# A hybrid RG-LRU, convolution, Fourier and SSD block: SSD by channels before the output projection, projections as slots between the stages

## The chip, the cores and the metric

The kernel runs on one core of a Trainium2 chip. The metric is the device time of one launch in microseconds (us). The engines are TensorE (PE in the profile, its weight loads PEld), VectorE (DVE), ScalarE (ACT), GpSimd (POOL) and SyncE (SP), on whose queue every DMA of both kernels is issued. SBUF holds 128 partitions; PSUM is used as eight banks of 128x512 float32, two to each of four names (`mm`, `tr`, `ba`, `bb`).

## The reference

2048 tokens of 1024 channels (x) and 256 context tokens (ctx), one layer. Both are normed and modulated, projected, handled by four branches of 512 channels, gated, concatenated and projected back:

```
h = rmsnorm(x) * (1 + scale) + shift          # scale, shift, gate = adaln(c)
rg_x, ssd_xbc, ssd_dt, rg_g, ssd_z, sc_b, sc_c, sc_x, sc_g, fn_x, fn_g = split(h @ w_in)
y_rg  = rglru(conv4(rg_x))                    # two directions, from the context's states
y_sc  = sc_b * conv3(sc_c * sc_x)             # in rows of 64 tokens
y_fn  = real(fft2(fn_x))                      # over tokens and 128 channels of 4 groups
# SSD: xs, B, C = silu(conv4(ssd_xbc)); dt = softplus(ssd_dt + bias); cs = cumsum(dt * a)
# in chunks of 128 tokens, 8 heads of 64 channels, 2 groups of B and C of 64 states, two directions:
y     = ((C B^T) * exp(cs_i - cs_j) masked) @ (xs * dt) + exp(cs) * (C @ entering state)
y_ssd = rmsnorm((y_fwd + y_bwd + D * xs) * silu(z)) * ssd_norm_w
out   = rmsnorm(x + gate * (concat(y_rg * silu(rg_g), y_sc * silu(sc_g),
                                   y_fn * silu(fn_g), y_ssd) @ w_out))
```

The context is projected for the RG-LRU, xbc and dt only, and gives the states from which the scans of the tokens start. Everything is float32.

## The kernel before, in words

Large products are made of three of reduced operands: `split` rounds a tile on ScalarE to a high part (`copy_hi`, the profile's L139) and subtracts it on VectorE or GpSimd for the low part (L214); `mm3` (L142 to L144) then issues high by high, high by low and low by high. `proj` makes a tile of 128 channels by 512 tokens in 24 such products from a weight block (`wload`) and the normed, transposed tokens `h_hi`, `h_lo`, which stay in SBUF.

The program text goes through the stages one after another: adaLN, the tokens `h`, and beside them the RG-LRU's input columns and the context's columns (`rgx_out`, raw columns to memory); the RG-LRU in units of 512 tokens, whose convolution stands in `rg_front` (L521 to L523) ahead of its gates' products; z and dt in token order, 128 tokens by 264 columns (`wz`); the xbc columns with convolution and silu (`conv_silu`, `xbc_emit`); the SSD's step sizes, decays and chunk states, of which the states from the right are passed on at this point (`states`, L678); Fourier mixing; the first SSD chunk; the short convolution; the gates; the output weights (`wo_raw`, `wo_hi`, `wo_lo`); and the output projection (`oproj`, L1153 to L1155), one block of 128 tokens after another.

The SSD's chunks are in token order. `ssd_head` computes the scores (L982), the decays from `ci`, a row of the cumulative sums broadcast to all partitions (L1022 to L1033), and the part of the entering state (L1004 and L1005, from `hs`); `ssd_tail` multiplies the masked scores `ma` with `xs` (L1044), adds, gates, norms the rows and transposes the result by TensorE (L1060) for the output projection. In the loop over the output's 16 token blocks `ssd_chunk` is called one block ahead (`NEARLY = 1`), so a chunk's head and tail lie between the products of blocks.

The kernel is built with `schedule_with_timeline_sim=True`: the program text gives the dependences and a preference, and a scheduler that simulates the engines sets the order of each engine's instructions. Buffers come from pools: a tile with `bufs=2` has two places, and a third use waits for the first one's readers. Each engine runs its instructions in the order so set.

## Time and profile before

| | |
|---|---|
| three runs | 1654.54, 1656.22, 1657.36 us (median 1656.22) |
| profiled execution, span | 1656.3 us |
| TensorE busy | 1569.4 us, 95% |
| VectorE busy | 1053.3 us, 64% |
| ScalarE busy | 714.9 us, 43% |
| GpSimd busy | 564.3 us, 34% |
| moved by DMA | 220.93 MB, mean 133 GB/s |

A row of the stage table gives the length of a stretch and then, engine by engine, how long it was busy in it; the clock behind it is the share of TensorE's full speed that was granted (1.0 is 2.4 GHz, 0.5 is 1.2 GHz). The timeline gives start and duration of instructions; since products overlap in TensorE's pipeline, the distance between two starts is the price of one, not its duration. A row of waits names the waiting instruction and the one it waited for.

### The profile page before, as it was taken

The numbers are of one execution on the slowest core, as the hardware profiler recorded it, in microseconds if no ns is written. First come the engines' busy times: TensorE is split into PE (matmuls) and PEld (weight loads), VectorE is DVE, ScalarE is ACT, GpSimd is POOL, SyncE is SP. The second block draws the span as 40 slices with busy tenths as digits, with TensorE's granted clock in tenths as the row PEclk, the third lists the DMA queues.
The fourth block names the chain that finished last, engine by engine and source line by source line (L and its number), as shares of the span: only waits on it lengthen the run. The fifth ranks groups of instructions, "written<-read, shape, count | busy, mean of one in ns | idle before, by whom it ended". The sixth has DMA issues, their size and how long they took to land. (4 is left out here: it accounts for less than half of the span.)

```text
span 1656.3 us, 22749 instructions
## 1 busy us (share of the span) xinstructions
PE 1569.4 (95%) x7906; PEld 1271.5 (77%) x7906; DVE 1053.3 (64%) x1837; ACT 714.9 (43%) x1383; POOL 564.3 (34%) x536
## 2 busy tenths in 40 slices
PE   6899999899899999899999999898988999999998
PEld 3687899777788778666788888785766777777787
DVE  7765354698986657644168653437468777878653
ACT  5654046557465536211222324424345544545432
POOL 5533123312211422343315345334423424243310
PEclk9999999999999999999999999999999999999999
DMA  8424232323332231454222236657575655555532
GB/s 328 153 87 135 87 99 92 106 90 104 124 116 71 83 121 58 148 156 128 77 79 61 87 109 179 174 161 233 165 254 171 183 146 171 146 170 148 162 105 70
DMA packets 182257, 220.93 MB, mean 133 GB/s; under 512 B 20183, under 2 KB 118905, under 8 KB 182142
## 3 DMA queue, kind: packets, MB, share of 16 engines
q1 hardware_dynamic: 182142, 219.48, 42.8%
q8 instruction: 62, 1.02, 0.3%
q14 instruction: 53, 0.43, 0.1%
HBM read 155.40 MB, written 64.03 MB: 132 GB/s over the span
## 5 line engine op out<-in xcount | busy, mean ns | idle before, releaser
L142 PE MATMUL ps_mm<-h_hi,whi 128*128 128x512 f32 x696 | 276.9, 401 | 5.6 <-ACT craw L347 4.5
L143 PE MATMUL ps_mm<-h_lo,whi 128*128 128x512 f32 x696 | 278.7, 400 | 1.8 <-DVE h_lo L309 1.0
L144 PE MATMUL ps_mm<-h_hi,wlo 128*128 128x512 f32 x696 | 278.3, 400 | 0.0
L142 PEld LDWEIGHTS ps_mm<-h_hi,whi 128*128 128x128 f32 x696 | 133.1, 192 | 36.2 <-ACT craw L347 5.4
L143 PEld LDWEIGHTS ps_mm<-h_lo,whi 128*128 128x128 f32 x696 | 133.3, 192 | 31.6 <-DVE h_lo L309 2.2
L144 PEld LDWEIGHTS ps_mm<-h_hi,wlo 128*128 128x128 f32 x696 | 133.6, 192 | 28.9 <-issue 1.4
L142 PE MATMUL ps_tr<-h_hi,whi 128*128 128x512 f32 x384 | 151.6, 395 | 0.0
L143 PE MATMUL ps_tr<-h_lo,whi 128*128 128x512 f32 x384 | 151.5, 395 | 0.0
L144 PE MATMUL ps_tr<-h_hi,wlo 128*128 128x512 f32 x384 | 151.1, 394 | 0.0
L1153 PE MATMUL ps_mm<-wo_hi,oyhl 128*128 128x512 f32 (+1 forms) x272 | 106.9, 393 | 7.5 <-ACT oyhl L139 7.5
L139 ACT ACTIVATE whi<-wraw 128x512 fp32r<-128x512 f32 (+1 forms) x77 | 49.6, 645 | 143.4 <-DMA wraw<-wblk 98.4
L1155 PE MATMUL ps_mm<-wo_hi,oyhl 128*128 128x512 f32 (+1 forms) x272 | 106.2, 391 | 2.8 <-DVE oyhl L214 2.7
L1154 PE MATMUL ps_mm<-wo_lo,oyhl 128*128 128x512 f32 (+1 forms) x272 | 106.9, 393 | 0.0
L1009 POOL TENSOR_TENSOR y<-y,e 128x256 f32<-128x256 f32 x32 | 35.6, 1114 | 195.3 <-DVE e L1008 195.3
L1154 PE MATMUL ps_tr<-wo_lo,oyhl 128*128 128x512 f32 (+1 forms) x256 | 100.4, 392 | 0.0
L1155 PE MATMUL ps_tr<-wo_hi,oyhl 128*128 128x512 f32 (+1 forms) x256 | 100.0, 390 | 0.0
L1153 PE MATMUL ps_tr<-wo_hi,oyhl 128*128 128x512 f32 (+1 forms) x256 | 99.1, 387 | 0.0
L214 POOL TENSOR_TENSOR wlo<-wraw,whi 128x512 fp32r<-128x512 f32 (+1 forms) x40 | 61.7, 1543 | 97.3 <-ACT whi L139 81.8
L142 PEld LDWEIGHTS ps_tr<-h_hi,whi 128*128 128x128 f32 x384 | 72.8, 190 | 16.8 <-issue 2.1
L143 PEld LDWEIGHTS ps_tr<-h_lo,whi 128*128 128x128 f32 x384 | 72.6, 189 | 16.4 <-issue 1.7
L144 PEld LDWEIGHTS ps_tr<-h_hi,wlo 128*128 128x128 f32 x384 | 72.6, 189 | 15.6 <-issue 1.1
L139 ACT ACTIVATE oyhl<-oyr 128x512 fp32r<-128x512 f32 x68 | 42.6, 627 | 96.2 <-PE ps_tr L1155 72.6
(365 smaller groups left out, 3847.9 us busy)
## 6 DMA issues: line engine op xcount, KB each, us to landing
wraw<-wblk SPq DMA_DIRECT2D x74, 256.0 KB, 3.0
oyr<-ycat SPq DMA_DIRECT2D x68, 256.0 KB, 3.4
ci<-cst_d SPq DMA_DIRECT2D x64, 256.0 KB, 3.5
xs<-xsb_d SPq DMA_DIRECT2D x31, 320.0 KB, 3.0
adar<-ada SPq DMA_DIRECT2D x16, 512.0 KB, 10.2
hf_d<-r_v SPq DMA_DIRECT2D x32, 256.0 KB, 2.2
ycat<-gy SPq DMA_DIRECT2D x32, 256.0 KB, 2.4
wo_raw<-wout SPq DMA_DIRECT2D x16, 512.0 KB
```

The source lines that it names most:

```text
L139: act.activation(dst, src, AF.Copy)
L142: pe.matmul(ps, wh, xh, start=start, stop=False)
L143: pe.matmul(ps, wh, xl, start=False, stop=False)
L144: pe.matmul(ps, wl, xh, start=False, stop=stop)
L214: eng.tensor_tensor(lo, raw, f32(hi), SUB)
L1009: pool.tensor_tensor(y[:, s], y[:, s], e[:, 0:256], ADD)
L1153: pe.matmul(p, yhl[:, 0, j], wo_hi[q][:, j, c0:c1], start=first and j == 0, stop=False)
L1154: pe.matmul(p, yhl[:, 0, j], wo_lo[q][:, j, c0:c1], start=False, stop=False)
L1155: pe.matmul(p, yhl[:, 1, j], wo_hi[q][:, j, c0:c1], start=False, stop=last and j == 3)
```

## The change

Seven things change.

- The RG-LRU's convolution moves from `rg_front` to `rgx_out`, so the start phase stores convolved columns `u_d`; `rg_front` only loads them.
- dt is made by channels from a small weight `wdt` (`dt_of`, both parts of the weight side by side in 32 columns). z is four more weight blocks whose tiles get the gate at once and go to `dz_d` by channels; `xbc_emit` stores `D * xs` beside them.
- The weight blocks behind the RG-LRU's and the context's, with their gates, become a list of `jobs` (the last two stand behind the chunks, as `lastgate` jobs of their own), and the generator `slots` gives one tile of 512 tokens after another. `along` takes the steps of a stage (RG-LRU, states, Fourier, chunks) and issues as many slots between them as the step's number says.
- `keep_in_program_order` exists for TensorE's instructions, but `inorder` is False throughout, so the scheduler sets TensorE's order as before.
- The states of both directions are passed on in one pass (`step`), and each chunk's entering states are stored (`hin_d`).
- The chunk is by channels (`Chunk`): the outputs are 64 channels by 128 tokens, two heads to a bank's upper and lower partitions; entering states come in as `er` by `hin`, where `er` is a broadcast row of `exp(cs)` times C; the norm's sum over channels is a product with ones, and its power goes back by a transpose. No transposes of the output are left.
- All chunks stand before the output projection; the pool of the output weights' raw tiles (`qy`) is opened after the chunks' pool is closed, and the first four token blocks go by weight quarters.

```diff
+        inorder = False
+        def matmul(self, *a, **k):
+            i = nc.tensor.matmul(*a, **k)
...
+    def rgx_out(p, n, blk, dst, at, end):
+        raw = qe.tile([128, 516], F32, name="ev", tag="ev", bufs=2)
+        act.activation(raw[:, 3:3 + n], p[:, :n], AF.Copy)
+        if at == 0:
+            pool.memset(raw[:, 0:3], 0.0)
+        else:
+            dve.tensor_copy(raw[:, 0:3], rgc[blk])
+        m = n
+        if at + n == end:
+            pool.memset(raw[:, n + 3:n + 4], 0.0)
+            m = n + 1
+        else:
+            dve.tensor_copy(rgc[blk], raw[:, n:n + 3])
+        wc = [cols[:, C_RGW + 4 * k + blk:C_RGW + 4 * k + blk + 1] for k in range(4)]
+        u = qe.tile([128, 516], F32, name="ru", tag="ru", bufs=1)
+        act.activation(u[:, 0:m], raw[:, 2:2 + m], AF.Identity, scale=wc[2], bias=cols[:, C_RGB + blk:C_RGB + blk + 1])
+        for k in (0, 1, 3):
+            dve.scalar_tensor_tensor(u[:, 0:m], raw[:, k:k + m], wc[k], u[:, 0:m], MUL, ADD)
+        o = int(at == 0)
+        st(dst[:, at - 1 + o:at - 1 + m], u[:, o:m])
+    def rgx(w, blk, hh, hl, n, dst, at, end):
+        rgx_out(proj(w, hh, hl, n, False), n, blk, dst, at, end)
...
+    def dt_of(hh, hl, n, c0):
+        m = n // 128
+        p = bank("ba")
+        for k in range(8):
+            pe.matmul(p[0:32, :n], dtw[:, k], hh[:, k], start=k == 0, stop=False)
+            pe.matmul(p[0:32, :n], dtw[:, k], hl[:, k], start=False, stop=k == 7)
...
+    def zgate(j):
+        def at(tt, w):
+            p = proj(w, h_hi[tt], h_lo[tt])
+            st(dz_d[tt][1, j], gate(p, q3))
+        return [(B_Z + j, at)]
...
+    jobs = [j for i in range(4) for j in zgate(i)]
+    jobs += [j for i in range(2) for j in shortconv(i)]
+    at_xbc = 4 * len(jobs)
+    jobs += [j for i in range(6) for j in xbc(i)]
+    jobs += [j for i in range(2, 4) for j in shortconv(i)]
+    jobs += [j for i in range(4) for j in lastgate(B_RGG + i, hf_d[i], i)]
+    jobs += [j for i in range(2) for j in lastgate(B_FNG + i, (yp_d, yq_d)[i // 2][i % 2], 8 + i)]
+    ready = [wload(jobs[0][0])]
+    def slots():
+        for i, (b, at) in enumerate(jobs):
+            w = ready.pop()
+            for tt in range(4):
+                at(tt, w)
+                if tt == 0:
+                    ready.append(wload(jobs[i + 1][0] if i + 1 < len(jobs) else B_FNG + 2))
+                done[0] += 1
+                yield
+    bulk = slots()
+    owed, done = [0.0], [0]
+    def upto(n):
...
+    def along(steps):
+        for n in steps:
+            owed[0] += n
+            while owed[0] >= 1:
+                owed[0] -= 1
+                next(bulk, None)
...
-        for blk, d, g, src, conv, keep, init in us:
-            if conv:
-                # two columns before and one after, zero beyond the ends
...
-                wc = [cols[:, C_RGW + 4 * k + blk:C_RGW + 4 * k + blk + 1] for k in range(4)]
-                dve.tensor_scalar(u[:, d, :n], e2[:, d, 2:2 + n], wc[2], cols[:, C_RGB + blk:C_RGB + blk + 1], MUL, ADD)
-                for k in (0, 1, 3):
-                    dve.scalar_tensor_tensor(u[:, d, :n], e2[:, d, k:k + n], wc[k], u[:, d, :n], MUL, ADD)
-                if keep is not None:
-                    st(keep, u[:, d, :n])
...
-            for b in range(16):
-                hh, hl = h_hi[b // 4], h_lo[b // 4]
-                s = slice(128 * (b % 4), 128 * (b % 4) + 128)
-                zp = mbank(True)
-                for k in range(8):
-                    mm3(zp[:, :264], hh[:, k, s], hl[:, k, s], *wzs[k], k == 0, k == 7)
-                zt = qz.tile([128, 264], F32, name="zt", tag="zt", bufs=2)
-                o = 8 * half
-                act.activation(zt, zp[:, 0:264], AF.Copy)
-                pool.tensor_copy(dtr[:, 2 + b, o:o + 8], zt[:, 256 * (1 - half):256 * (1 - half) + 8])
-                st(z_d[b][:, 256 * half:256 * half + 256], zt[:, o:o + 256])
...
-        mas = []
-        for g in range(2):
-            cs2 = []
-            for d in range(2):
-                ci = sd.tile([128, 4, 128], F32, name="ci", tag="ci", bufs=3)
...
+            ci = d2("ci", (4, 2, 128), bufs=3)
+            ld(ci, cst_d[rows].rearrange("h d i -> (h d i)")[None, :].partition_broadcast(128)
+               .rearrange("p o (h d i) -> p (o h) d i", d=2, i=128))
+            er = d2("er", (4, 128))
+            for d in range(2):
+                ld(er[64 * d:64 * d + 64], ecst_d[d, rows].rearrange("h i -> (h i)")[None, :].partition_broadcast(64)
...
+            pool.tensor_tensor(ci, ci, cs_[:, c, :, hs].rearrange("p d h -> p h d")[:, :, :, None]
+                               .to_broadcast([128, 4, 2, 128]), SUB)
+            ma, m1 = ci[:, :, 0], ci[:, :, 1]
+            act.activation(m1, m1, AF.Relu, scale=-1.0)
+            dve.scalar_tensor_tensor(ma, ma, 0.0, m1, MIN, SUB)
+            act.activation(ma, ma, AF.Exp)
+            pool.tensor_tensor(er, er, b4(self.cc2[:, g]), MUL)
...
+        def outputs(self, g):
+            if g == 0:
+                self.yp = bank("bb").rearrange("p (j i) -> p j i", j=4)
+            for j in range(2):
+                for l, r, first in ((self.xs, self.ma[g], True), (self.hin, self.er[g], False)):
+                    for e in range(2):
+                        at = 64 * (4 * g + 2 * j + e)
+                        pe.matmul(self.yp[64 * e:64 * e + 64, 2 * g + j], l[:, at:at + 64], r[:, 2 * j + e],
+                                  start=first, stop=not first)
+        def gated(self):
+            c, so = self.c, self.so
+            yz = d2("yz", (2, 4, 128), bufs=2)
+            ld(yz, dz_d[c // 4][:, :, :, so].rearrange("i b c t -> c i b t"))
+            y, gz = self.y, _ = yz[:, 0], yz[:, 1]
+            dve.tensor_tensor(y, y, self.yp, ADD)
+            dve.tensor_tensor(y, y, gz, MUL)
+            act.activation(gz, y, AF.Square)
+            self.sq = d2("sq", (128,), bufs=1)
+            dve.tensor_reduce(self.sq, gz.rearrange("p j t -> p t j"), mybir.AxisListType.X, ADD)
+        def scale(self):
+            p = bank("ba")
+            pe.matmul(p[:, 0:2], self.sq, ones2, start=True, stop=True)
+            rs = one("srs")
+            dve.tensor_scalar(rs, p[:, 0:1], 0.25 / 512, EPS, MUL, ADD)
+            pool.tensor_tensor(rs, rs, mhalf, ALU.pow)
+            self.rs = rs
+        def normed(self):
+            p = bank("ba")[:, 0:128]
+            pe.transpose(p, self.rs.to_broadcast([128, 128]), ident)
+            dve.scalar_tensor_tensor(self.y, self.y, 0.5, b4(p), MUL, MUL)
+            st(ycat[self.c // 4][12:16, :, self.so].rearrange("b c t -> c b t"), self.y)
+    def chunk_steps(per):
+        cur, prev = Chunk(0), None
+        cur.scores()
+        cur.decays(0)
+        cur.decays(1)
+        yield 2.5
+        for c in range(16):
+            nxt = Chunk(c + 1) if c < 15 else None
+            yield per / 2
+            if prev:
+                prev.scale()
+            if nxt:
+                nxt.scores()
+            cur.outputs(0)
+            if nxt:
+                nxt.decays(0)
+            yield per / 2
+            cur.outputs(1)
+            cur.gated()
+            if prev:
+                prev.normed()
+            if nxt:
+                nxt.decays(1)
+            prev, cur = cur, nxt
+        yield 1
+        prev.scale()
...
+    qye = ExitStack()
+    qy = qye.enter_context(pool_of("qy", right))
+    op0 = [[bank("mm"), bank("tr")] for _ in range(2)] + [[bank("ba"), bank("bb")] for _ in range(2)]
+    for q in range(4):
+        for b in range(4):
+            oproj(yhl_of(b, q), q, op0[b], halves, q == 0, q == 3)
...
-            if b + NEARLY < 16:
-                ssd_chunk(b + NEARLY)
```

What the scheduler makes of it is read from the orders. On TensorE before, in the output projection's loop, a chunk's scores (`cct`, `bt`) and outputs (`xs`, `ma`) stand between products of the output weights (`wo_hi`, `wo_lo`) with a token block's split outputs `oyhl`:

```order
L1153 MATMUL ps_tr<-wo_hi_10804,oyhl 128x512
L1154 MATMUL ps_tr<-wo_lo_10805,oyhl 128x512
L1155 MATMUL ps_tr<-wo_hi_10804,oyhl 128x512
L982 MATMUL ps_ba<-cct,bt 128x128 x2
L1044 MATMUL ps_bb<-xs,ma 128x64 x8
L1153 MATMUL ps_mm<-wo_hi_10654,oyhl 128x512
L1154 MATMUL ps_mm<-wo_lo_10655,oyhl 128x512
L1155 MATMUL ps_mm<-wo_hi_10654,oyhl 128x512
```

After, in the same engine's order, in the last eleven of the sixteen chunks, `cct` by `bz` are the next chunk's scores, `ones` by `sq` and `ident` by `srs` the norm, `ci` (now the masked scores) by `xs` and `er` by `hin` the outputs:

```order
L129 MATMUL ps_ba<-ones_9283,sq 128x2
L129 MATMUL ps_ba<-cct,bz_9285 128x128 x2
L133 MATMUL ps_ba<-ident,srs 128x128
L129 MATMUL ps_bb<-ci,xs 64x128 x2
L129 MATMUL ps_bb<-er,hin 64x128 x2
L129 MATMUL ps_bb<-ci,xs 64x128 x2
L129 MATMUL ps_bb<-er,hin 64x128 x2
L129 MATMUL ps_bb<-ci,xs 64x128 x2
L129 MATMUL ps_bb<-er,hin 64x128 x2
L129 MATMUL ps_bb<-ci,xs 64x128 x2
L129 MATMUL ps_bb<-er,hin 64x128 x2
```

The products of the projections and of the output projection that stood between two chunks' instructions are gone from here. Of the 256 products that give the chunks' outputs, 80 are issued when the last product of a projection is; from there on the order holds only rows as these, eleven chunks of them, and then the output projection. The products of 512 columns in the projections rise from 3264 to 3648; the 768 of 264 columns go.

On SyncE's queue before, the last gates' loads (`gy`) and stores and the output weights' loads (`wo_raw`) alternate:

```order
L134 DMA gy<-yq_d 128x512
L134 DMA ycat_149<-gy 128x512
L134 DMA gy<-yq_d 128x512
L134 DMA wo_raw<-wout 128x1024
L134 DMA oyr<-ycat_147 128x4x128
L134 DMA ycat_150<-gy 128x512
L134 DMA gy<-yq_d 128x512
L134 DMA ycat_147<-gy 128x512
L134 DMA wo_raw<-wout 128x1024 x2
L134 DMA gy<-yq_d 128x512
L134 DMA wo_raw<-wout 128x1024
```

After, at the end of the chunks, `er`, `hin` and `yz` are the last chunks' loads and `ycat` from `yz` their stores:

```order
L146 DMA er<-ecst_d 64x512 x2
L146 DMA ycat_134<-yz 128x4x128
L146 DMA hin<-hin_d_159 128x512
L146 DMA er<-ecst_d 64x512 x2
L146 DMA yz<-dz_d_130 128x8x128
L146 DMA ycat_134<-yz 128x4x128 x2
L146 DMA wo_raw<-wout 128x1024 x4
L146 DMA oyr<-ycat_131 128x4x128 x3
L146 DMA wo_raw<-wout 128x1024 x4
```

Here the output weights' loads have moved behind the last chunk's store; all sixteen stand there.

## Rows read from the trace of the kernel before

**Rows 1.** The page: span, and busy time of each engine.

```profile
span 1656.3 us, 22749 instructions
PE 1569.4 (95%) x7906; PEld 1271.5 (77%) x7906; DVE 1053.3 (64%) x1837; ACT 714.9 (43%) x1383; POOL 564.3 (34%) x536
```

**Rows 2.** Stretches of the span: length, engines' busy us, PEclk, DMA share, GB/s.

```profile
0.00:200.00 200.00, 176.69 (x1024) 142.09 (x1025) 117.82 (x217) 94.53 (x164) 80.36 (x95) 0.99 0.46 160
200.00:700.00 500.00, 469.47 (x2368) 398.15 (x2366) 358.57 (x522) 260.32 (x391) 139.41 (x141) 0.97 0.31 101
700.00:1050.00 350.00, 349.16 (x1852) 281.68 (x1853) 177.69 (x277) 94.69 (x202) 142.55 (x115) 0.99 0.38 113
1050.00:1300.00 250.00, 224.81 (x998) 174.42 (x997) 153.73 (x293) 109.14 (x247) 95.06 (x84) 0.95 0.65 194
1300.00:1600.00 300.00, 300.00 (x1402) 232.90 (x1401) 223.23 (x492) 142.92 (x352) 101.73 (x95) 1.00 0.52 153
1600.00:1656.00 56.00, 49.29 (x270) 42.32 (x269) 22.27 (x40) 13.30 (x29) 5.21 (x6) 0.96 0.26 85
```

**Rows 3.** Waits of TensorE: us in total, times, longest.

```profile
PE ps_ba L142 <- DVE uh L531: 11.7, 5, 5.0
```

**Rows 4.** TensorE in time: start, us, instruction; z's products, then projections.

```profile
217.10 0.28 PE L143 MATMUL ps_mm<-wz_lo,h_hi 128*128 128x264 f32 x1
...
219.64 0.29 PE L143 MATMUL ps_mm<-wz_lo,h_hi 128*128 128x264 f32 x1
...
420.45 0.40 PE L142 MATMUL ps_mm<-h_hi,whi 128*128 128x512 f32 x1
...
423.88 0.39 PE L142 MATMUL ps_mm<-h_hi,whi 128*128 128x512 f32 x1
```

**Rows 5.** TensorE in time: one SSD chunk between products of the output projection.

```profile
1329.04 0.49 PE L982 MATMUL ps_ba<-cct,bt 64*128 64x128 f32 x4
...
1331.27 0.48 PE L1153 MATMUL ps_mm<-wo_hi,oyhl 128*128 128x512 f32 x1
...
1335.12 0.65 PE L678 MATMUL ps_ba<-xw,xs 128*64 128x256 f32 x4
1335.71 0.50 PE L1004 MATMUL ps_ba<-hs,ch 128*128 128x512 f32 x1
...
1336.57 0.50 PE L1154 MATMUL ps_tr<-wo_lo,oyhl 128*128 128x512 f32 x1
```

**Rows 6.** Groups by shape: busy us, mean ns | idle before them, releaser.

```profile
L339 DVE SCALAR_TENSOR_TENSOR cu<-craw,ssw,cu 128x512 f32<-128x512 f32 x72 | 56.2, 796 | 2.7 <-POOL gl L214 1.4 <-ACT cu L337 1.0
...
L1024 ACT ACTIVATE ci<-ci,pk 128x128 f32<-128x128 f32 x128 | 41.1, 391 | 36.3 <-DMA ci<-cst_d 36.3
...
L1028 ACT ACTIVATE ci<-ci 128x512 f32<-128x512 f32 x32 | 20.2, 632 | 32.5 <-DVE ci L1027 32.5
...
L671 POOL TENSOR_TENSOR xw<-xs,pk 128x512 f32<-128x512 f32 x19 | 20.9, 1105 | 31.4 <-DMA xs<-xsb_d 15.0 <-PE ps_bb L730 7.8 <-DVE pk L719 5.1
...
L1056 POOL TENSOR_TENSOR srs<-srs,mhalf 128x1 f32<-128x1 f32 x16 | 15.5, 972 | 13.2 <-DVE srs L1055 10.7 <-DMA ci<-cst_d 2.6
...
L214 POOL TENSOR_TENSOR wo_lo<-wo_raw,wo_hi 128x1024 fp32r<-128x1024 f32 x3 | 7.6, 2520 | 2.7 <-ACT wo_hi L139 2.7
```

**Rows 7.** ScalarE in time: `ci` of two successive SSD chunks.

```profile
1128.52 1.28 ACT L1024 ACTIVATE ci<-ci,pk 128x128 f32<-128x128 f32 x4 [4.66 <-DMA ci<-cst_d]
...
1141.55 1.28 ACT L1024 ACTIVATE ci<-ci,pk 128x128 f32<-128x128 f32 x4 [2.41 <-DMA ci<-cst_d]
```

**Rows 8.** One stretch, columns as in rows 2.

```profile
1120.00:1140.00 20.00, 17.07 (x65) 12.45 (x65) 13.56 (x34) 10.45 (x26) 7.40 (x7) 0.83 0.88 267
```

**Rows 9.** DMA issues: KB each, median us from issue to landing.

```profile
ci<-cst_d SPq DMA_DIRECT2D x64, 256.0 KB, 3.5
...
xr<-x SPq DMA_DIRECT2D x16, 512.0 KB, 4.0
...
ycat<-yt SPq DMA_DIRECT2D x16, 256.0 KB, 3.8
```

More of the change, by code (lines that the diff above doesn't have):

```diff
@@ L776, in build, with channels @@
     ld(ft, A["ftab"])
-    for kind in range(2):
+    def channels(kind, first):
         nk = 260 if kind == 0 else 256
@@ L780, in build, with weights @@
         wh, wl = [], []
-        for k in range(8):
+        op = ADD if kind == 0 else SUB
+        def weights(k):
             wt = fo.tile([128, 4, 128], F32, name="wft", tag="wft", bufs=2)
@@ L837, in build @@
             st(znd, zt[0:1])
+    for kind in range(2):
+        along(channels(kind, kind == 0))
     f4.close()
```

762 lines of the change are left out of this document (356 added, 406 removed).

## The prediction

> **What bounds the kernel now.** I read the busy times and the span first, then the span cut by stages, then what TensorE waits for, and last the timelines of the engines that serve the SSD chunks. TensorE works in 95% of the span [rows 1], so only its 86.9 us of idle time and the time at a lowered clock can be won without taking work away. The stage table [rows 2] shows where they lie: 23.3 us idle before 200 us (adaLN, normed tokens), 30.5 between 200 and 700, 0.8 up to 1050, 25.2 between 1050 and 1300 (first SSD chunks beside the gates and the output weights), nothing between 1300 and 1600, and 6.7 at the very end. The granted clock adds (1 - clock) x length: 250 us at 0.95 lose 12.5 us, 500 at 0.97 lose 15, 350 at 0.99 lose 3.5. So 200 to 1300 holds about 56.5 us idle and 31 us of clock, 87 in all. The reader is to see above all the row from 1300 to 1600: there the output projection runs with an SSD chunk for every 128 tokens between its products, VectorE is busy for 223 of 300 us and ScalarE for 143, and TensorE does not wait once. The chunks' long work off TensorE is hidden by the output projection.
>
> The sum is made against the profiled execution, 1656.3 us, which is also the median of the runs.
>
> **A, the start phase: +5 us (0 to +25).** The RG-LRU's convolution goes into the start phase: for 20 tiles two ScalarE passes and three of VectorE's multiply-adds (0.63 and 0.80 us a piece [rows 6]) in place of one copy. That is 25 us more on ScalarE (94.5 of 200 us busy) and some 35 more on VectorE (117.8 of 200 [rows 2]). Both fit beside TensorE's 176.7 if they are spread; the convolved tile has one buffer, so at worst VectorE's surplus over the 23.3 us of idle time and the last tiles' tail show. I take 5, nearer to the covered case.
>
> **B, TensorE's own work: +10 us (-5 to +45).** z and dt in token order go: 768 products of 264 columns; their rows stand 2.54 us apart over 21 products, 0.121 us each [rows 4], so -92.9. z by channels is 384 more products of 512 columns; 15 of them take 3.43 us, 0.229 each [rows 4], so +87.8. dt alone is 64 products, 32 rows by 512 columns; priced by the same row, +14.6. A chunk's own products: before, scores and outputs take 2.23 us (from 1329.04 to 1331.27) and the entering states' part 0.86 (from 1335.71 to 1336.57) [rows 5], and four transposes; the states' products (from 1335.12 on) stay in number and move ahead. After, it is 16 products `64x128` in pairs, two scores, one small product and one transpose. No row shows such a pair; the nearest is the states' pair of 256 columns, 0.59 us (1335.12 to 1335.71 [rows 5]): 0.30 by its half, 0.59 if the columns did not count. So 8 pairs with the rest take 2.9 to 5.2 us; I take 3.5, which with three transposes fewer is level with before. Sum 9.5, called 10.
>
> **C, the stalls between 200 and 1300: -45 us (-75 to -10).** Projections now stand between the steps of RG-LRU, states and Fourier stages. The wait for `uh`, 11.7 us [rows 3], has projections to fill it and a faster engine for the conversion; the stretch 1050 to 1300, 25.2 + 12.5 = 37.7 us [rows 2], is another stretch now, with projections and no chunks that wait for loads. That makes 49.4; I leave 4 for waits that stay, since each slot's eviction now stands on the same ScalarE and VectorE as the stage it fills. The ends: -75 if nearly all of the 87 go, -10 if new waits for the slots' own evictions appear.
>
> **D, the chunks without cover: +87 us (+48 to +138).** The scheduler, and not the generator of the slots, sets TensorE's order, and it puts the projections early: the last of them stands where only 80 of the 256 chunk-output products have been issued. The other 176 are 11 chunks, one behind the other with nothing between, as the rows of TensorE's order in the change show. The output projection stands behind all sixteen, since its weights' loads do. There TensorE waits, and a chunk costs its period. Its bounds:
> - GpSimd has two subtractions of 128x1024 (2.52 us each by the nearest row of that shape), two 128x512 products with a broadcast (1.10) and a power (0.97) [rows 6]: 8.2 us.
> - ScalarE has sixteen 128-column scalings (0.39) and five passes of 512 (0.63) [rows 6]: 9.4 us.
> - DMA: a chunk brings 3.0 MB into SBUF and out (two broadcasts of 512 KB, two of 256 KB, z and D's part 512 KB, inputs and output the rest). Between 1050 and 1300 194 GB/s took a share of 0.65 [rows 2], so 298 GB/s at a full queue: 10.1 us. A 512 KB load lands after 4.0 us, a 256 KB one after 3.5 [rows 9].
> - The kernel before shows the same chain with little cover: `ci`'s four steps on ScalarE begin at 1128.52 and, a chunk later (two halves), at 1141.55, 13.0 us apart, waiting for the load of `ci` [rows 7].
> - The upper end adds the subtraction on GpSimd, which stands in this chain now, 2.5 us: 15.5.
>
> Three engines and the queue lie within 2 us of one another, and they work in a chain (load, subtract, Relu, Min, Exp, scale, multiply, product, gate, square, sum, power, transpose), with one `hin`, one `gm` and one `m0`. I take 12, nearer to the row of the kernel before than to the busiest engine. 11 x 12 = 132, less half a chunk prepared in advance (6) and the chunks' own products, which are in B (11 x 3.5 = 38.5): 87.5. With 9 it is 54 (48 with a chunk in advance), with 16 it is 131 (138 without any).
>
> **E, behind the last chunk: +16 us (+8 to +25).** The last chunk's sum of squares, power, transpose, scaling and store (about 6 us by the durations above, a store's 3.8 [rows 9] beside other work) has no product beside it, and the first output weights are loaded (512 KB, 4.0 us [rows 9]), converted and subtracted (2.5 us [rows 6]) only then, since their buffers lie in the chunks' memory: about 10 for four of them until TensorE can keep going. Before, these loads ran beside the last projections.
>
> 5 + 10 - 45 + 87 + 16 = +73: **1729 us**.
>
> **The clock.** Between 1120 and 1140 TensorE was busy for 17.07 of 20 us, in pieces with gaps between, and the granted clock was 0.83 [rows 8]: a third of that stretch at 1.2 GHz. In the bare stretch TensorE works 3.5 of 12 us, far less. The Trainium skill (TensorE: Matmul & The Clock Gate, Part 1) puts it so: "the default state is throttled, and activity releases the throttle"; its section on why this matters for kernels advises against idle gaps between bursts of matmuls. By that rule the whole stretch would run at half the clock; the row agrees in direction, and no row here shows a stretch as empty as this one.
>
> **Rivals.**
> 1. *Faster.* The cover was not worth as much as I think: the chunks run at the rate of the busiest engine, 9 us, the two-sided overlap hides half of E, A and B come out at nothing, and the stalls of the middle go nearly all. 11 x 9 - 6 - 38.5 = 54.5; 54.5 + 8 - 75 = -12.5: 1644 us. With the same C and E it decides at a period of 10.1 us. For it: the engines' sums are 8.2 to 9.4. Against it: 10.1 for the transfers and 13.0 seen.
> 2. *Half clock on the chain.* TensorE's 3.5 us a chunk become 7 at 1.2 GHz; since outputs, gate, power, transpose and the next outputs follow one another in TensorE's order, they lengthen the period to about 16. D becomes 131: 1773 us. For it rows 8; against it, that chunks can overlap TensorE's part with the next one's loads.
> 3. *The start phase gets longer* by the whole of VectorE's surplus, +25 for +5: 1749 us. Against it: VectorE's and ScalarE's shares there.
> 4. *The recast does not do what it says*, should the projections reach into the last chunks after all: then D shrinks by 8.5 us for each chunk covered, and the time comes out as rival 1's. The order speaks against it.
>
> **How the numbers follow.** Main case 0.58, rival 1 with 4 0.14, rival 2 0.20, rival 3 0.08. The main case's own range is 1695 to 1760 (D's period from 10 to 14 gives -22 and +22, C and B the rest). The time should lie between 1650 and 1795 8 times in 10: the low end takes in most of rival 1, the high end rival 2 with a slow start. Within 0.2% (3.3 us) is about what a measurement of this kernel cannot tell from no change; such a result needs rival 1 with a period of 10.1 and little else: 0.03. Faster 0.14, slower 0.83.
>
> **What would show it.** The page after must have a trough of TensorE of three to four of the 40 slices (130 us or so) behind the last projection, at a granted clock near 0.5, with GpSimd, ScalarE, VectorE and DMA busy, and then an output projection at full busy share with no chunk in it. ScalarE's Exp passes there must come 6 us apart (two a chunk). The conversions of the output weights must all lie behind the trough. The slices of 1050 to 1300 must be full before it. I am wrong if TensorE is busy for 9 tenths in that stretch, if a chunk's period is under 10 us, or if the middle stages wait as long as before.

## The result, and the profile after

The changed kernel takes 1777.99 us (1774.33 to 1779.62, four runs), the kernel before 1655.38 in the same session: 1.0747 of its time, 95% interval 1.0718 to 1.0775. It is slower, as forecast, by 122.6 us where 73 were forecast: inside the range of 1650 to 1795 us, but above the 1695 to 1760 that the prediction gave its main case. The profiled execution's span grew from 1656.3 to 1772.5 us, by 116.2.

The page, where the first line of busy times is followed by three of its rows of 40 slices (busy tenths of TensorE, the granted clock, the share of the DMA engines):

```profile
span 1772.5 us, 22088 instructions
PE 1592.4 (90%) x7770; PEld 1267.1 (71%) x7770; DVE 982.0 (55%) x1508; ACT 742.5 (42%) x1393; POOL 500.9 (28%) x424
...
PE   6899999899997799999999999999444499999998
...
PEclk9999999999998899999999999999555599999999
DMA  7332132323232334554322365697978733322322
```

The trough of TensorE that was asked for is there: four slices (44 us each) at 4 tenths, with the clock at 5 and the DMA engines at 7 to 9, and behind it the output projection at 9. The first five stages of [rows 2], same columns:

```profile
0.00:200.00 200.00, 172.88 (x947) 132.31 (x948) 146.40 (x269) 112.39 (x188) 78.16 (x95) 0.97 0.40 145
200.00:700.00 500.00, 464.06 (x2058) 376.01 (x2056) 291.86 (x433) 287.48 (x431) 98.16 (x74) 0.97 0.32 101
700.00:1050.00 350.00, 350.00 (x1814) 273.60 (x1813) 196.25 (x275) 88.46 (x176) 126.58 (x103) 1.00 0.40 124
1050.00:1300.00 250.00, 201.53 (x1101) 161.05 (x1099) 145.80 (x230) 119.56 (x311) 130.61 (x98) 0.86 0.77 224
1300.00:1600.00 300.00, 238.43 (x1100) 189.14 (x1101) 147.63 (x213) 103.33 (x224) 61.01 (x45) 0.82 0.51 158
```

Before 1050 us nothing was won: 27, 36 and 0 us idle in the first three rows against 23, 31 and 1 before. From 1050 to 1600 there are 110 us idle against 25. What TensorE waited for, in total, times, longest:

```profile
PE ps_bb L129 <- DVE ci L1187: 48.5, 11, 7.3
PE ps_ba L129 <- DVE sq L1210: 14.4, 6, 6.6
PE ps_bb L133 <- DVE craw L365: 13.2, 1, 13.2
PE ps_mm L129 <- ACT oyhl L151: 11.1, 1, 11.1
PE ps_tr L129 <- ACT craw L360: 10.4, 1, 10.4
PE ps_ba L133 <- POOL srs L1217: 10.3, 10, 2.1
```

The masked scores (`ci`, L1187), the sum of squares and the power are the chunks' results; the two rows of `craw` are something else, one wait each, and `uh` of [rows 3] is down from 11.7 to 5.8 us. Four stretches, columns as in rows 2: the seam behind the RG-LRU; the last stretch with projections, whose last product ends at 1242.5 us; the bare chunks, up to the last chunk's sum of squares; and from there to the first product of the output projection:

```profile
550.00:620.00 70.00, 46.04 (x188) 35.95 (x187) 46.58 (x84) 38.16 (x56) 11.45 (x11) 0.83 0.27 89
1100.00:1250.00 150.00, 133.95 (x704) 106.46 (x703) 88.07 (x134) 70.10 (x180) 81.71 (x58) 0.94 0.77 226
1249.50:1391.50 142.00, 62.55 (x404) 47.24 (x404) 104.78 (x158) 78.55 (x211) 77.09 (x51) 0.50 0.81 230
1391.50:1404.40 12.90, 0.97 (x3) 0.59 (x3) 3.86 (x5) 4.80 (x5) 2.40 (x2) 0.50 0.78 249
```

In the third, TensorE is busy for 63 of 142 us at a granted clock of 0.50 all through; [rows 8] had 0.83 in its worst 20 us. It holds ten and a half chunks, 13.5 us each. GpSimd's powers, one to a chunk (11 from the first to the last of these rows, so 13.3 us apart; [rows 7] had 13.0):

```profile
1251.81 0.99 POOL L1217 TENSOR_TENSOR srs<-srs,mhalf 128x1 f32<-128x1 f32 x1
...
1384.70 0.98 POOL L1217 TENSOR_TENSOR srs<-srs,mhalf 128x1 f32<-128x1 f32 x1 [1.64 <-DVE srs L1216]
```

To put the 116 us to the terms of the sum, I took for every product the distance to the next start, less the usual distance of its kind, and added up by stretches; this sum of lost time counts idle time and half clock alike. Lost in all: 123.5 us before, 242.9 after. These are estimates from the traces: what is usual is a choice, and another one moves A, B and C by a few us each.

| term | forecast | measured | from |
|---|---|---|---|
| A, start phase | +5 | +7 | lost up to 200 us: 29.5, now 36.9 |
| B, TensorE's own work | +10 | -3 | the spans' difference less that of the losses |
| C, stalls from 200 to the bare stretch | -45 | -13 | 90.3, now 77.1 |
| D, bare chunks | +87 | +112 | 1249.4 to 1391.4 |
| E, behind the last chunk | +16 | +15 | 1391.4 to 1412 |
| the rest of the output projection | 0 | -2 | 3.7, now 2.0 |

The border between C and D is a choice too. Counted from the end of the last projection, 1242.5, another 6 us go from C's losses to D's: C is then about -20 and D +118.

### The profile page after: what moved, and what is told of

It reads as the page before. It is cut to its first block, busy times and chain, and to the rows that moved or that the text cites. A ratio compares the mean times of both kernels' runs of the same rounds, so it can differ in the third digit from the quotient of the medians.

```text
span 1772.5 us, 22088 instructions
## 1 busy us (share of the span) xinstructions
PE 1592.4 (90%) x7770; PEld 1267.1 (71%) x7770; DVE 982.0 (55%) x1508; ACT 742.5 (42%) x1393; POOL 500.9 (28%) x424
## 4 chain that ended last, share of the span: by engine, by line
PE 63%; DVE 11%; DMA 10%; ACT 7%; issue 4%; POOL 3%; SPq 1%; POOLq 0%; ACTq 0%; DVEq 0%
PE ps_mm L129 26%; PE ps_tr L129 23%; PE ps_bb L129 7%; PE ps_ba L129 6%; DMA wraw<-wblk 2%; DVE r_v L703 2%; DMA er<-ecst_d 2%; SPq L146 1%; DVE m L1186 1%; DMA ci<-cst_d 1%; DVE r_v L700 1%; DVE ada L293 1%; ACT r_e L752 1%; DMA u_d<-ru 1%; DMA yq_d<-fvr 1%
## 5 line engine op out<-in xcount | busy, mean ns | idle before, releaser
L129 PE MATMUL ps_tr<-h_hi,whi 128*128 128x512 f32 x544 | 217.7, 400 | 10.4 <-ACT craw L360 10.4
L129 PE MATMUL ps_tr<-h_hi,wlo 128*128 128x512 f32 x544 | 216.6, 398 | 0.0
L129 PE MATMUL ps_tr<-h_lo,whi 128*128 128x512 f32 x544 | 216.1, 397 | 0.0
L129 PE MATMUL ps_mm<-wo_hi,oyhl 128*128 128x512 f32 (+1 forms) x480 | 181.6, 390 | 11.1 <-ACT oyhl L151 11.1
L226 DVE TENSOR_TENSOR oyhl<-oyr,oyhl 128x512 fp32r<-128x512 f32 x68 | 48.5, 716 | 156.0 <-ACT oyhl L151 156.0
L129 PEld LDWEIGHTS ps_tr<-h_hi,whi 128*128 128x128 f32 x544 | 104.3, 192 | 34.5 <-ACT craw L360 10.9
L129 PEld LDWEIGHTS ps_tr<-h_lo,whi 128*128 128x128 f32 x544 | 104.1, 191 | 23.2 <-issue 2.8
L129 PEld LDWEIGHTS ps_tr<-h_hi,wlo 128*128 128x128 f32 x544 | 103.9, 191 | 23.0 <-issue 2.0
L129 PEld LDWEIGHTS ps_mm<-wo_hi,oyhl 128*128 128x128 f32 x480 | 89.3, 188 | 32.4 <-ACT oyhl L151 11.4
L129 PEld LDWEIGHTS ps_tr<-wo_hi,oyhl 128*128 128x128 f32 x448 | 83.2, 188 | 19.0
```

Of the source, the lines that this page charges most:

```text
L129: i = nc.tensor.matmul(*a, **k)
L226: eng.tensor_tensor(lo, raw, f32(hi), SUB)
```

## The experiments

All start from the changed kernel. Theory 1 is the prediction's: what costs the time is missing cover, that is, that TensorE has no other products to run beside the chunks. It had to be mended twice on the way. Ratios are to the kernel before.

**e1, the text's order.** TensorE's instructions keep the order of the program text, so that projections and chunks alternate to the end.

```diff
-    pe.inorder = False
+    pe.inorder = True
```

> The changed kernel with TensorE's instructions kept in the order of the program text from the slots on, so that 24 to 48 projection products stand ahead of each of the 16 chunks and 192 behind the last, where the output weights are loaded. Theory 1 (the loss is the missing cover: the scheduler put the projections ahead of the last 11 chunks): a chunk of some 13 us gets 5.5 to 11 us of products, the stretch behind the last chunk is covered, the granted clock in the chunk stretch rises well above 0.5; 1700 us (1680 to 1725). Theory 2 (the chunk by channels is bound by its own transfers and engines wherever it stands, and the projections only move): 1760 or more. Rival: waits that the text's order brings in the RG-LRU and Fourier stages eat the gain, 1740 to 1790, with waits outside the chunk stretch.

Measured: 1857.24 us, 1.124 (1.1209 to 1.1272). Only theory 2's open end ("1760 or more") holds this time. The 285 us from the first score to the last output, and TensorE's largest wait:

```profile
1151.00:1436.00 285.00, 189.29 (x1098) 152.59 (x1100) 166.03 (x259) 140.67 (x365) 154.46 (x104) 0.81 0.72 215
```

```profile
PE ps_ba L129 <- DVE sq L1210: 65.7, 9, 10.9
```

TensorE has more work beside the chunks there, but in the text the sum of squares' product stands right behind the outputs it needs, and everything behind it waits for VectorE, nine times and up to 10.9 us. Over the whole program the losses rise to 324.7 us. But that wait is not what makes e1 slower than the changed kernel, whose chunks stood bare instead: from 1100 us on e1 loses only some 14 us more. The larger part arises where the rival had it, at the waits that the text's order brings to earlier stages. From 200 to 550 us TensorE is busy for 314 of 350 us, at a clock of 0.94 (338 in the changed kernel, at 1.00), and from 700 to 1044 for 318 of 344, also at 0.94 (344, at 1.00); by the sums of lost time some 34 us more in each. So the scheduler's order is not bad as such: with the same pieces, the text's is 80 us worse. The form of theory 1 that blames the scheduler for drawing the projections ahead falls.

**e2 and e3, the chunks back between the output projection's blocks.** Chunk `b + 1` is issued inside block `b`; the weights' raw tiles move out of the chunks' memory and come in halves (two tiles of 2 KB a partition), since the chunks' pool now stays open. Two more things differ from the changed kernel, here and in e6, e8 and e12: `ci` has two buffers in place of three, and the first four token blocks go one by one, through the banks `mm` and `tr` alone, and not by weight quarters through all eight. e3 has the text's order as well.

```diff
-    along(chunk_steps(1.15))
+    AHEAD = 1
+    along(next(chunks) for at_step[0] in range(1, 6 + 2 * AHEAD - 1))
...
+                    if q in (1, 3):
+                        advance(...)    # the steps of chunk b + 1
                     oproj(yhl_of(b, q), q, op_, cs, q == 0, q == 3)
```

> The changed kernel with all but the first chunks back between the output projection's token blocks (one block ahead), the chunks themselves by channels as in the change, two buffers for ci, the output weights loaded beside the last gates in halves; the scheduler sets the order. In it three chunks and a half stand without products instead of ten and a half. Theory 1: seven chunks of 13 us less their own 3.5 to 5 come back, and the tail behind the last chunk: 1680 us (1665 to 1700). Theory 2 (chunks are bound by themselves): the blocks of the output projection stretch beyond their 22 us and the time stays over 1740.

> As e2, with TensorE kept in the text's order: no chunk stands without products, the projections lie together ahead of the output projection. Theory 1: TensorE has no bare stretch, 1640 us (1625 to 1665), which would beat the kernel before. Rival: the text's order brings waits for a chunk's result inside the output projection's blocks, a few us a block, 1680 to 1720.

Measured: e2 1728.17 us, 1.0461 (1.0435 to 1.0486); e3 1811.26, 1.0973 (1.0949 to 1.0996). e2 wins half of what was expected. Its 96 us from the last projection to the first product of the output projection:

```profile
1224.00:1320.00 96.00, 25.54 (x182) 20.27 (x182) 56.43 (x84) 46.95 (x109) 39.80 (x28) 0.54 0.85 235
```

There 42% of the chain of waits (followed back from each instruction to what released it) is the loads of the output weights through the small tiles, an obstacle of my own edit; e3 shows it as one wait for the first split outputs, in which the chain of waits runs through load, conversion and subtraction of one small tile after another (e3 also has e1's waits in the earlier stages):

```profile
PE ps_mm L129 <- ACT oyhl L151: 50.4, 1, 50.4
```

**e4, idle products in the bare stretch.** The text is written as the scheduler had it, and behind each half chunk from the seventh chunk on stand products that nobody reads.

```diff
+            if self.c >= 6:
+                fill = bank(("mm", "tr")[g])
+                for _ in range(3):
+                    pe.matmul(fill, ident, self.ma[g].rearrange("p h i -> p h i"), start=True, stop=True)
```

> The changed kernel with the text written as the scheduler had it (projections ahead of chunk 6) and, from chunk 6 on, three idle float32 products of 128x512 behind the products of each half chunk, whose result nobody reads; they depend on the half's masked scores. Theory 3 (the half clock lies on the chunks' chain): the clock goes to 1.0 there, the period falls from 12.6 to 10 us or less and the time to 1745 (1735 to 1755). Theory 1 (the chain of load, subtraction, Relu, Min, Exp, scalings and sums sets the period, TensorE's part is small): the period moves by under 1 us, 1765 to 1785. If the clock stays at 0.5 the fill itself makes TensorE the bound: above 1790.

Measured: 1798.24 us, 1.0892 (1.086 to 1.0923, two runs). The bare stretch:

```profile
1250.00:1300.00 50.00, 29.98 (x144) 16.97 (x145) 31.40 (x46) 22.84 (x62) 22.05 (x15) 0.76 0.73 220
...
1350.00:1400.00 50.00, 31.78 (x155) 17.13 (x154) 29.89 (x46) 25.81 (x70) 28.76 (x20) 0.86 0.67 200
```

The clock rose to 0.76 to 0.86, not to 1.0, and the chunks did not come faster; the stretch grew by 23 us. Theory 3 as put falls. It does not say what the half clock alone costs, since the fill also stood in the chunks' way: its products are 18% of the chain of waits from 1250 us to the last outputs. The changed kernel's chain of waits gives a bound: 17.3% of 143 us, 25 us, are TensorE's products on the chain at 1.2 GHz, so at 2.4 GHz some 12 us less by this estimate, if nothing else came late.

**e5, a gate at the seam.** Where the RG-LRU's memory is given up, the xbc convolution's tiles wait; four tiles of a gate that needs none of that memory go first.

```diff
+    jobs += lastgate(B_RGG, hf_d[0], 0)
     jobs += [j for i in range(6) for j in xbc(i)]
```

> The changed kernel with the four tiles of the first RG-LRU gate moved in the list of slots to stand ahead of the xbc blocks, at the seam where the RG-LRU's memory is given up. In the changed kernel TensorE loses some 28 us there (10.4 and 13.2 us of waits for the xbc convolution's tiles, the rest at the half clock). If these products fill the seam: 1757 us (1748 to 1766). Rival: the scheduler draws them ahead into the RG-LRU anyway and the seam stays bare: 1772 to 1783.

Measured: 1780.64 us, 1.0788 (1.0768 to 1.0808): no gain. The same two stretches as the first two of the changed kernel above:

```profile
550.00:620.00 70.00, 61.30 (x264) 49.25 (x263) 44.25 (x76) 34.88 (x52) 17.10 (x13) 0.98 0.28 93
1100.00:1250.00 150.00, 118.37 (x613) 91.37 (x613) 82.05 (x132) 66.35 (x175) 76.41 (x55) 0.90 0.75 217
```

The seam is filled: 61.3 of 70 us busy at clock 0.98, in place of 46.0 at 0.83. The second stretch gave it all back: 118.4 of 150 in place of 134.0, at 0.90 in place of 0.94. Neither expectation saw that: the gain was real where it was made and was lost where those four tiles had lain before. By the sums of lost time, with the same usual distances for both runs, some 19 us fewer at the seam, 20 more from 1100 to 1249 and 6 more in what follows.

**e6 and e8, the weights through larger tiles.** As e2, with three tiles of 4 KB, two of them the weight block that has done its last gate, for which the last two gates come one after the other; e8 adds e5's edit.

```diff
-                r = qr.tile([128, 512], F32, name="wo_raw", tag="wo_raw", bufs=2)
+            if k == 0:
+                r = qr.tile([128, 1024], F32, name="wo_raw", tag="wo_raw", bufs=1)
+            else:
+                r = wp.tile([128, 1024], F32, name="wo_raw", tag=f"w{('hi', 'lo')[k - 1]}{free}")
```

> As e2 (chunks between the output projection's blocks, the scheduler's order), but the output weights come through three buffers of 4 KB a partition, two of them from the weight block that is free, and not through two of 2 KB. One and a half chunks stand without products. Theory 1 in the form that e1 leaves it (what hides a chunk is a block of the output projection, 22 us, longer than a chunk's period; a slot or two of projections is not): 1670 us (1655 to 1690). Rival: the chunk by channels also stalls between blocks, and the weights' loads still stand bare: 1700 to 1720.

> e5 and e6 together. If the seam and the bare chunks are separate losses the gains add: e6's time less 15 to 22 us, 1652 us (1635 to 1670), within 1% of the kernel before; if the order is reshuffled by the one and the other, e6's time.

Measured: e6 1690.27 us, 1.0241 (1.0219 to 1.0262), the best of the changed forms; e8 1697.95, 1.0282 (1.0256 to 1.0307), so the seam's gain is given back here too. e6 from the last projection to the first output product, and on to the last chunk:

```profile
1222.00:1272.00 50.00, 14.70 (x106) 11.50 (x106) 34.34 (x42) 27.12 (x52) 21.91 (x15) 0.57 0.96 298
1272.00:1632.00 360.00, 349.04 (x1762) 281.25 (x1762) 195.40 (x317) 139.16 (x347) 87.12 (x69) 0.97 0.59 172
```

Inside the output projection TensorE is busy for 349 of 360 us with the outputs of eleven chunks in it: a block of 96 products hides a chunk by channels nearly as well as it hid the old one [rows 2]. What is left bare, 50 us, are chunks and weights together ahead of the first block.

**e7, half of the load of `ci`.** Two heads' rows are loaded and serve four, so the decays of the other two heads are left out. The expectation calls everything else unchanged, but `ci` has two buffers in place of three, and GpSimd's subtraction comes in two instructions.

```diff
-            ci = d2("ci", (4, 2, 128), bufs=3)
+            ci = d2("ci", (4, 2, 128), bufs=2)
+            cl = d2("cl", (2, 2, 128), bufs=2)
+            ld(cl, ...)    # 256 KB in place of 512
+            for b in range(2):
+                pool.tensor_tensor(ci[:, 2 * b:2 * b + 2], cl, ..., SUB)
```

> The changed kernel with half the load of ci: two heads' rows are loaded and serve four, so the decays of the other two heads are left out; everything else is issued as before (the subtraction in two instructions). A chunk moves 2.4 MB in place of 2.9. If the transfers set the period in the bare stretch (DMA share 0.81): the stretch from the last projection to the last chunk, 142 us, becomes 118 and the time 1752 (1745 to 1760). If the chain over the engines sets it: under 8 us, 1768 to 1780.

Measured: 1772.17 us, 1.0738 (1.0702 to 1.0774, two runs). The changed kernel and then e7, each in two parts of the bare stretch:

```profile
1246.00:1300.00 54.00, 22.32 (x140) 17.07 (x140) 37.24 (x56) 29.47 (x80) 30.92 (x21) 0.50 0.91 254
1300.00:1392.00 92.00, 42.38 (x271) 31.94 (x271) 70.13 (x104) 51.29 (x138) 48.69 (x33) 0.50 0.75 213
```

```profile
1246.00:1300.00 54.00, 19.45 (x137) 15.31 (x139) 37.80 (x58) 28.89 (x78) 31.18 (x27) 0.56 0.76 226
1300.00:1392.00 92.00, 41.57 (x272) 31.98 (x268) 66.87 (x101) 49.24 (x135) 54.05 (x45) 0.50 0.60 170
```

The DMA share falls from 0.91 and 0.75 to 0.76 and 0.60, and the last outputs come 4.6 us sooner. So the fullness of the queue does not set the period. Single loads still may: what GpSimd no longer waits for `ci` it waits for `er`, from 1246 to 1398 us 32.8 us in 14 waits, against 10.9 in 6 in the changed kernel; and the edit has a buffer of `ci` fewer.

**e9, the norm without its way over TensorE and GpSimd.** The product with ones, the power and the transpose are left out; the scaling multiplies by a mask that is there.

```diff
-            pe.matmul(p[:, 0:2], self.sq, ones2, start=True, stop=True)
-            pool.tensor_tensor(rs, rs, mhalf, ALU.pow)
-            pe.transpose(p, self.rs.to_broadcast([128, 128]), ident)
```

> The changed kernel without the way of the norm over TensorE and GpSimd: the product with ones, the power and the transpose are left out, and the scaling multiplies by a mask that is there (so the norm is left out; the squares and their sum are still made). e7 showed that the transfers do not set the chunk's period of 13 us. If the loop outputs, gate, square, sum, power, transpose, next outputs sets it, as TensorE's transpose stands ahead of the next chunk's products: the period falls to 10 or 11 and the time to 1750 (1740 to 1760). Rival: the decays' own chain (load, subtraction, Relu, Min, Exp, scalings, sum, product) with its buffers sets it: 1768 to 1778.

Measured: 1780.43 us, 1.0796 (1.077 to 1.0823, two runs). With less work the last outputs come 9.4 us later. The stretch from 1246 us to them:

```profile
1246.00:1398.00 152.00, 53.75 (x372) 40.07 (x372) 100.41 (x146) 77.78 (x211) 69.75 (x41) 0.51 0.71 211
```

The norm's loop alone does not set the period either. But its place was taken at once: the loads of `ci` landed after 9.0 us (median) where they had landed after 5.6, and they are 23.5% of e9's chain of waits in this stretch, 9.0% in the changed kernel's. GpSimd's waits for them from 1246 to 1398 us, in the changed kernel and in e9:

```profile
POOL ci L1170 <- DMA ci<-cst_d: 30.7, 15, 7.1
```

```profile
POOL ci L1170 <- DMA ci<-cst_d: 55.5, 14, 7.3
```

e7 and e9 each take out one link, another one takes over, and the period stays. That fits several loops of nearly one length better than a single cause, but no run takes out two at once. What sets the period, the loads, the decays' steps or their buffers, stays open.

**e10 and e11, more products beside the chunks.** No slots in the Fourier stages and two or three beside each chunk, the text's order from the first chunk on, and the norm's sum later in it; e11 adds e5's edit and has 2.2 slots a chunk in place of 2.4.

```diff
-                yield 0.42
+                yield 0
...
+    pe.inorder = True    # behind the Fourier stages
-    along(chunk_steps(1.15))
+    along(chunk_steps(2.4))
```

> The changed kernel with no slots in the Fourier stages, so that 24 more of them are left, two or three (48 to 72 products) to each chunk and 264 products behind the last; TensorE keeps the text's order from the first chunk on alone, and the norm's sum stands a half chunk later in it. Theory 1 in its third form (the chunks take 15 us each from the first score to the last output whatever lies beside them, 241 us in the changed kernel, 237 in e7; what counts is how many products lie beside them and not before): Fourier ends 130 us sooner, the chunk stage takes 260 to 280 us, nothing is bare behind it: 1680 us (1660 to 1705). Rival (as e1 could be read: products beside the chunks lengthen a chunk by as much as they cover): the chunk stage takes over 340 us, 1740 or more.

> As e10, with e5's gate at the seam, which no longer robs the chunks of products that they need. Theory 1: e10's time less 15 to 20 us, 1662 us (1640 to 1690). Rival: the gain at the seam is given back elsewhere again, e10's time.

Measured: e10 1790.2 us, 1.0852 (1.0833 to 1.0871); e11 1793.96, 1.0884 (1.0863 to 1.0906). The Fourier stage and the chunks, in the changed kernel and then in e10 at the same times:

```profile
750.00:1022.00 272.00, 272.00 (x1440) 213.78 (x1439) 162.76 (x226) 60.41 (x121) 101.66 (x78) 1.00 0.36 111
1044.00:1363.00 319.00, 236.37 (x1318) 187.67 (x1317) 197.90 (x305) 158.49 (x414) 170.55 (x125) 0.80 0.78 224
```

```profile
750.00:1022.00 272.00, 205.26 (x1101) 156.24 (x1100) 163.16 (x245) 78.16 (x182) 103.24 (x93) 0.88 0.39 118
1044.00:1363.00 319.00, 288.07 (x1580) 231.81 (x1580) 186.28 (x288) 154.90 (x391) 171.74 (x116) 0.93 0.71 211
```

Beside the chunks it worked: 288 of 319 us busy at clock 0.93, and no bare stretch, though the chunks themselves took longer, 319 us where theory 1 had 260 to 280 and the rival over 340. But the Fourier stage, full before, stood without its slots at 205 of 272 us and clock 0.88. By the sums some 128 us more are lost from 700 to 1050 than in the changed kernel, and 108 fewer from there on. What covers the chunks here was taken from a stage that had used it. The four programs have the same 7770 products, so their losses over the whole program differ as their spans do: 1772.5 us in the changed kernel, 1779.3 in e5, 1789.1 in e10 and 1790.8 in e11. Wherever the projections were put, the sum did not fall; it grew by 7, 17 and 18 us.

**e12, the memory, with the chunks first in the text.** All sixteen chunks stay ahead of the output projection in the text, and the scheduler is free; the chunks' pool stays open, and the output weights have tiles of their own, as in e6. With that go e6's other edits: two buffers of `ci`, the token blocks one by one, and the last two gates one after the other.

```diff
-    sdp.close()
...
-            r = qy.tile([128, 1024], F32, name="wo_raw", tag="wo_raw", bufs=4)
+    qy = qye.enter_context(pool_of("qy", right))    # behind the weights' loads
...
-    op0 = [[bank("mm"), bank("tr")] for _ in range(2)] + [[bank("ba"), bank("bb")] for _ in range(2)]
```

> The changed kernel with all sixteen chunks still ahead of the output projection in the text, but the output weights in memory of their own (one tile of 4 KB and the free weight block's two) while the chunks' pool stays open to the end; two buffers for ci, token blocks one by one. The scheduler, free as in the change, then draws the output projection's products beside the chunks: about two and a half chunks stand bare, the last nine have 57 to 80 products of the output projection each. Theory (the filler is a fixed amount, and what the change gave away is the output projection's, by putting the weights' tiles where the chunks' lie): 1695 us (1680 to 1710), near e6. Rival (that the text has the chunks first is what counts): over 1740.

Measured: 1715.01 us, 1.0385 (1.0341 to 1.043), 5 us over the expected range and 63 us under the changed kernel. The bare stretch, then the chunks with output products:

```profile
1240.00:1296.00 56.00, 18.44 (x117) 14.14 (x117) 47.16 (x55) 33.55 (x74) 30.12 (x17) 0.55 0.96 294
1296.00:1484.00 188.00, 170.41 (x924) 133.29 (x924) 120.17 (x198) 90.64 (x233) 69.53 (x50) 0.96 0.75 211
```

The scheduler now draws the output projection's products beside the last nine chunks, busy for 170 of 188 us at clock 0.96. That the chunks come first in the text is not the cause of these 63 us; that nothing of the output projection could start before they were through, is. Two ties held it back, and e12 loosens both: the memory of `qy`, and the chunks' banks `ba` and `bb`, which the first four token blocks asked for. In the changed kernel's trace it is the memory that is waited for: the first load into `qy` starts at 1394.6 us, 0.5 us behind the last chunk's last pass on VectorE. Whether the banks alone would have held the products back was not tried.

## Why the prediction came out as it did

- **The direction and its cause were right** (D): eleven chunks with no product between, at half clock, the output projection behind them. The mechanism is confirmed by e6 and e12, which give the chunks the output projection's products again (with the small edits named there) and win 88 and 63 us.
- **D was too small by 25 us**, inside its own range. The period was taken at 12 and is 13.5, as near to the 13.0 of [rows 7] as the trace of before could say: 16 us in ten and a half chunks. And the chunks' own products count 2.8 us a chunk at full clock, not 3.5, so less is to be taken off: 8 us, and part of why B is 13 below its value. Half a chunk did lie in advance: its outputs start at 1242.4 us, directly behind the last projection. A pair of products takes 0.22 us at full clock, less than the 0.30 taken from [rows 5], and twice that at half clock; starts of two such pairs, beside projections and in the bare stretch:

```profile
1163.49 0.39 PE L129 MATMUL ps_bb<-er,hin 128*64 128x128 f32 x4
1163.71 0.39 PE L129 MATMUL ps_bb<-ci,xs 128*64 128x128 f32 x4
...
1297.34 0.64 PE L129 MATMUL ps_bb<-er,hin 128*64 128x128 f32 x4
1297.77 0.64 PE L129 MATMUL ps_bb<-ci,xs 128*64 128x128 f32 x4
```

- **The step that failed is C** ("-45 us", from "projections to fill it"): 13 us were won, near the weak end of its range. One of the prediction's own signs of being wrong came with it, "if the middle stages wait as long as before": from 200 to 1050 us TensorE is idle for 36 us, before for 31. The waits in the RG-LRU did go, 28.8 us lost from 200 to 550 before, 12.2 now. Two things were missed. At the seam where the RG-LRU's memory passes to the xbc stage 29.2 us are lost in place of 8.6. And the stretch of 1050 to 1300, whose 37.7 us I let go, was not emptied: the first five chunks moved into it, and from 1100 to 1249 it still loses 26.6 us (some 6 of them behind the last projection). Behind both is an assumption that the sum never stated: that every product put into a stall is a gain. e5, e8, e10 and e11 show that it is none while a later stage lives on the same products. The projections were filler already used up; what the change gave away is the output projection's own. The time came out inside the range because that range was wide: the two misses, in C and in D, point the same way, and only B's is against them.
- **Rival 2** names 1773 us, close to the time, but that is luck, for its reason is not what the runs show. Its clock is there; its period of 16 is not, and e4 brought the clock up to 0.8 without a gain, though with products of its own in the way. The trace has a granted clock of 0.50 through the whole bare stretch, with TensorE busy for 63 of 142 us. The Trainium skill (TensorE: Matmul & The Clock Gate, Part 1) has the throttled state as the default, which activity lifts; the trace agrees.
- **Rivals 1, 3 and 4** did not come. The busiest engine's 9 us were no bound that the chunks reached: VectorE, the busiest there, worked for 105 of 142 us. That is 10.0 us a chunk, more than the 8.2 and 9.4 that the prediction had for GpSimd and ScalarE; its bounds leave VectorE out. The start phase cost 7.4, near the forecast. The order did what it said.
- **E** was right (15 for 16): the weights' loads and conversions all lie behind the last chunk.
- **No form beats the kernel before.** The nearest is e6, 2.4% slower; by the sums it still loses some 28 us at the seam, 42 from the last projection to the first output product, and 21 behind that.

## What to carry to other kernels

Products that may run anywhere are a fixed amount; before moving them into a stall, find the stage that will lack them, and count the cover of the whole program, not of the place. In this kernel the long chain of small steps off TensorE belonged beside the products that are bound to come last, since nothing else could use these. And when a scheduler is free to interleave, look for what forbids it: here buffers shared by two stages, above all one pool in another's memory, and not the order of the text.

## What the runs showed of the hardware

VectorE's passes of 128x512 with two operands in SBUF lengthen while GpSimd works through its long ones. In the bare stretch of the changed kernel the gate's product (L1207, both operands in SBUF) takes 0.68 us beside an idle GpSimd and 1.35 to 2.36 beside a working one, and the sum of the scaled scores (L1186) 1.5 us on average and up to 2.4; the addition of the outputs (L1206, one operand in PSUM) takes 0.69 even beside it. VectorE, then GpSimd, in the same 17 us:

```profile
1302.10 0.68 DVE L1207 TENSOR_TENSOR yz<-yz 128x512 f32<-128x512 f32 x1
...
1312.73 0.69 DVE L1206 TENSOR_TENSOR yz<-yz,ps_bb 128x512 f32<-128x512 f32 x1 [1.23 <-PE ps_bb L129]
...
1315.09 1.35 DVE L1207 TENSOR_TENSOR yz<-yz 128x512 f32<-128x512 f32 x1
```

```profile
1299.37 1.26 POOL L1177 TENSOR_TENSOR er<-er,cct 128x512 f32<-128x512 f32 x1
...
1305.71 1.91 POOL L1170 TENSOR_TENSOR ci<-ci,pk 128x1024 f32<-128x1024 f32 x1 [5.08 <-ACT m L1184]
...
1312.31 1.91 POOL L1170 TENSOR_TENSOR ci<-ci,pk 128x1024 f32<-128x1024 f32 x1 [2.06 <-DMA ci<-cst_d]
1314.17 1.71 POOL L1177 TENSOR_TENSOR er<-er,cct 128x512 f32<-128x512 f32 x1
```

The Trainium skill (GPSIMD Engine Reference, section 1, Specifications) says that GpSimd shares its SBUF interfaces with VectorE, with contention where a VectorE instruction has two SBUF inputs; these rows agree, for the spared PSUM operand too. GpSimd's own instructions from 1246 to 1410 us, against [rows 6]: the subtraction of 128x1024 took 1.94 us where I had taken 2.52, the product 1.43 where I had taken 1.10.

```profile
L1170 POOL TENSOR_TENSOR ci<-ci,pk 128x1024 f32<-128x1024 f32 x20 | 38.8, 1938 | 42.5 <-DMA ci<-cst_d 30.7 <-ACT m L1184 9.2 <-PE ps_bb L129 2.6
...
L1177 POOL TENSOR_TENSOR er<-er,cct 128x512 f32<-128x512 f32 x21 | 29.9, 1426 | 12.4 <-DMA er<-ecst_d 10.9 <-PE ps_bb L129 1.2 <-POOL ci L1170 0.2
```

The broadcast loads, too, land later than I had taken from [rows 9]: after 5.6 us for 512 KB, and 4.6 for 128 KB, where a load of 512 KB that is no broadcast took 4.0 and a broadcast of 256 KB 3.5. That the fuller queue does it (a share of 0.81 in the bare stretch) is not shown: in e7, at 0.60 to 0.76, the 128 KB still landed after 4.4.

```profile
ci<-cst_d SPq DMA_DIRECT2D x32, 512.0 KB, 5.6
...
er<-ecst_d SPq DMA_DIRECT2D x64, 128.0 KB, 4.6
```
